# First pointwise product of a two-block transformer step: a new order for its operands, the diagonals and the first norm sums

## The chip, the core and the metric

The kernel runs on one core of one Trainium2 chip. A core has a matrix engine (TensorE, PE in the rows; PEld is its weight load), a vector engine (VectorE, DVE), an activation engine (ScalarE, ACT), a general engine (GpSimd, POOL) and an engine that here only issues transfers (SyncE, SP). Each works through its own instructions in the order in which the program was written, and they wait for each other by semaphores. The metric is device microseconds of one execution. Before the change three runs took 1481.81, 1485.37 and 1486.15 us, the median is 1485.37 us.

## The reference, cut to what matters

The program computes two blocks on 256 positions of 1024 channels in fp32. All that the change touches lies in the opening of the first block:

```python
c_act = silu(c)
mod = c_act @ mod_w + mod_b                      # 6 x 1024: shifts, scales, gates
sh_m, sc_m, gt_m, sh_f, sc_f, gt_f = split(mod)
h = rmsnorm(x, norm_pre_mix) * (1 + sc_m) + sh_m # x * rsqrt(mean(x^2) + eps) * g
u = h @ a_pw1_w + a_pw1_b                        # 1024 -> 2048, "first pointwise product"
a, gt = split(u)
u = a * sigmoid(gt)
u = causal_dwconv(u, a_dw_w) + a_dw_b            # 31 taps, depthwise
u = silu(layernorm(u, a_ln_g, a_ln_b))
x = x + gt_m * rmsnorm(u @ a_pw2_w + a_pw2_b, norm_post_mix)
...                                              # conv feed-forward, then the second block
```

## The kernel before

Everything is held with channels on the 128 partitions, in eight channel tiles of 256 positions (`xr` is x, `ys` work space). Products keep fp32 accuracy with two fp32r parts: an operand is split into a high part (a rounded copy) and a low part (the rest), and three matmuls high x high, high x low and low x high are summed. Weights come as 1 MB chunks (`wraw`, three buffers, `Stream.load`, L200). Each half chunk is split by ACT (`whi`, L226) and DVE (`wlo`, L235); when the second half has been split, SP is given the load of the chunk three further on (L238 to L241).

`pointwise_conv` (L915) is the opening. It goes like this:

- **Start.** PE runs matmuls that have no use but activity (`keep_warm`, L923; `WARM_START`, L31, says how many at four places), two matmuls that spread silu(c) over the partitions (L933), then more of the first kind. ACT squares x (L939); DVE adds the eight squared tiles up pairwise (L942 to L950), and two matmuls with one column sum over the partitions (L953). ACT and DVE make one over the root (L957, L975), PE transposes it (L977), ACT copies it to `rms` (L982).
- **Modulation.** One column of mod for a channel tile is a row of `mod_w` (`mraw`, 512 KB, five buffers) times silu(c) on DVE (`mod_mult`, L720) and a sum along the row on ACT (`mod_sum`, L724, an instruction and the readout of its accumulator). Each input tile k of the product needs two, shift and scale (`mult` and `sums`, L960 and L966). ACT's sum frees the buffer, and SP then loads a later row.
- **Product.** For each input tile k, PE does 48 matmuls (`pw1`, L1004): eight output tiles, two halves, three parts, into all eight PSUM banks. Its operand is made by DVE (`scaled`, L985, x times gain times rms), by DVE's add of a bias (L1031), by ACT (scale and shift, L1033; high part, L1034) and DVE (low part, L1045), and its weights by two splits.
- **Other work in the loop.** After k = 1 SP is given `taps` (L1051), the convolution's coefficients. After k = 2 POOL is given five instructions (`conv_stack`, L901) that each make 32x32 diagonal matrices of one channel tile out of the taps. After k = 5 SP is given `vecs`, the biases and gains, and `cst` (`load_consts`, L662).
- **Convolution.** ACT takes a sigmoid of each gate (L1099, with a bias out of `vecs`), DVE multiplies (`up`, L1101). PE makes shifted copies (L1072), ACT moves them (`sh`, L1076), and PE multiplies them with the diagonals (L1128) for seven channel tiles; the eighth is done by DVE, tap by tap (L1084, L1088). Between the taps DVE works on the 24 later rows of `mod_w`, ACT sums them; these are queued in `bg` and issued by `pump` while the convolution is written down. At its end come layer norm sums and the second pointwise product.

The order of all this is the order of the code: no scheduler moves anything. A DVE instruction that is written after a PE instruction does not wait for it unless it uses its data or a buffer that it holds.

## Time and profile before

| | |
|---|---|
| median of three runs | 1485.37 us |
| the profiled execution | 1481.87 us |
| its span (first to last instruction) | 1480.1 us |
| PE busy in the span | 1419.9 us (96%) |
| DVE, ACT, POOL busy | 1076.0, 853.8, 119.6 us |
| mean granted TensorE clock | 0.978 |

Of the span PE is busy nearly throughout, but the change is confined to the first 130 us. There the rows below are read: a timeline row gives the start, the busy time, the engine, the line of the code, the operation, output <- input and the number of instructions of a run; a bracket at its end gives the idle time of the engine before it and what ended it. A window row gives for a stretch its length, the busy time of engines, the granted clock of TensorE (1.00 is 2.4 GHz, 0.50 is 1.2 GHz), the share of the DMA engines' time and GB/s.

### The profile page before, as it was taken

Reading aid. Unit: us, or ns where it says so; the run is one execution under the profiler, and the core shown is the slowest. Engines: PE = TensorE matmul, PEld = TensorE weight load, DVE = VectorE, ACT = ScalarE, POOL = GpSimd, SP = SyncE. Lnnn points to the kernel's source line nnn. Section 1 sums busy time; section 2 is a strip of 40 time slices with the busy share of each in tenths; the row PEclk is TensorE's granted clock in tenths of the full one; section 3 lists DMA queues with packets and bytes.
Section 4 is the critical chain, followed back from the end, with each engine's and each line's share of the span. In section 5 each row is a group of like instructions: output and inputs, shape, how many; then the busy total and the mean of one; then the engine's idle time right before and its main releaser. Section 6 shows DMA issues by size and latency. Waiting matters only on the chain. (4 is left out here: it accounts for less than half of the span.)

```text
span 1480.1 us, 26075 instructions
## 1 busy us (share of the span) xinstructions
PE 1419.9 (96%) x10664; PEld 1273.4 (86%) x10664; DVE 1076.0 (73%) x1705; ACT 853.8 (58%) x1505; POOL 119.6 (8%) x113
## 2 busy tenths in 40 slices
PE   8888899999999999999999999999999999999997
PEld 7867799998888888898788888888888888888886
DVE  7897788885777656788568776678766765787754
ACT  6787566684655535751346555466554676565542
POOL 1210100001000010031010000110001111100011
PEclk9998899999999999999999999999999999999998
DMA  9774445565355553240024555536554342265540
GB/s 379 292 243 186 170 155 189 198 234 207 136 202 179 196 199 136 86 143 4 2 109 167 184 196 181 189 143 221 182 195 187 136 143 86 91 226 196 196 174 29
DMA packets 39145, 250.38 MB, mean 169 GB/s; under 512 B 4337, under 2 KB 4849, under 8 KB 12274
## 3 DMA queue, kind: packets, MB, share of 16 engines
q1 hardware_dynamic: 38594, 247.60, 45.9%
q8 instruction: 84, 1.38, 0.4%
q10 hardware_dynamic: 432, 1.11, 0.2%
q14 instruction: 35, 0.29, 0.1%
HBM read 247.65 MB, written 1.05 MB: 168 GB/s over the span
## 5 line engine op out<-in xcount | busy, mean ns | idle before, releaser
L235 DVE TENSOR_TENSOR wlo<-wraw,whi 128x1024 fp32r<-128x1024 f32 x416 | 514.3, 1250 | 34.1 <-ACT whi L226 33.4
L226 ACT CAST whi<-wraw 128x1024 fp32r<-128x1024 f32 x416 | 426.3, 1045 | 22.0 <-PE acc L378 5.6
L384 PE MATMUL acc<-hx,whi 128*128 128x512 f32 x880 | 310.7, 398 | 0.0
L384 PE MATMUL acc<-xx,whi 128*128 128x512 f32 x816 | 284.1, 390 | 0.0
L372 PE MATMUL acc<-xx,wlo 128*128 128x256 f32 x1008 | 280.7, 284 | 0.0
L372 PE MATMUL gu<-xx,wlo 128*128 128x256 f32 x1008 | 279.0, 282 | 1.6 <-ACT xx L625 1.0
L372 PE MATMUL acc<-hx,wlo 128*128 128x256 f32 x880 | 247.5, 281 | 0.0
L384 PEld LDWEIGHTS acc<-hx,whi 128*128 128x128 f32 x880 | 165.3, 188 | 40.5
L372 PEld LDWEIGHTS gu<-xx,wlo 128*128 128x128 f32 x1008 | 189.9, 189 | 4.9 <-ACT xx L625 1.7
L372 PEld LDWEIGHTS acc<-xx,wlo 128*128 128x128 f32 x1008 | 190.9, 191 | 0.8
L384 PEld LDWEIGHTS acc<-xx,whi 128*128 128x128 f32 x816 | 153.2, 188 | 32.1
L372 PEld LDWEIGHTS acc<-hx,wlo 128*128 128x128 f32 x880 | 166.1, 189 | 0.0
L384 PE MATMUL gu<-xx,whi 128*128 128x512 f32 x432 | 150.9, 390 | 0.0
L377 PE MATMUL gu<-xx,whi 128*128 128x256 f32 x512 | 148.4, 290 | 2.4 <-ACT u L894 2.4
L378 PE MATMUL gu<-xx,whi 128*128 128x256 f32 x512 | 142.9, 279 | 0.0
L1331 ACT ACTIVATE ys<-ys 128x256 f32<-128x256 f32 (+1 forms) x66 | 28.6, 437 | 151.7 <-DVE ys L1249 134.9
L377 PEld LDWEIGHTS gu<-xx,whi 128*128 128x128 f32 x512 | 96.2, 188 | 10.8 <-issue 7.9
L378 PEld LDWEIGHTS gu<-xx,whi 128*128 128x128 f32 x512 | 96.3, 188 | 0.7 <-issue 0.7
L384 PEld LDWEIGHTS gu<-xx,whi 128*128 128x128 f32 x432 | 81.1, 188 | 17.0
L1348 POOL TENSOR_TENSOR nsum<-ys 128x512 f32<-128x512 f32 (+1 forms) x9 | 12.4, 1380 | 871.1 <-PE acc L384 452.3
L858 ACT COPY lows<-acc 128x256 f32<-128x256 f32 x55 | 20.6, 374 | 97.8 <-PE acc L384 97.6
L1247 DVE SCALAR_TENSOR_TENSOR ys<-xr,acc 128x256 f32<-128x256 f32 x32 | 13.5, 422 | 75.0 <-PE acc L384 75.0
(397 smaller groups left out, 2351.5 us busy)
## 6 DMA issues: line engine op xcount, KB each, us to landing
wraw<-in_w SPq DMA_DIRECT2D x208, 1024.0 KB, 4.8
mraw<-in_mod SPq DMA_DIRECT2D x48, 512.0 KB, 5.5
xr<-in_x SPq DMA_DIRECT2D x2, 512.0 KB, 4.2
m<-in_mem SPq DMA_DIRECT2D x1, 1024.0 KB, 8.2
out<-xr SPq DMA_DIRECT2D x3, 256.0 KB, 2.2
cst<-in_consts SPq DMA_DIRECT2D x1, 546.0 KB
lora<-in_lora ACTq DMA_DIRECT2D x1, 384.0 KB, 3.4
lora_g<-in_lora ACTq DMA_DIRECT2D x1, 384.0 KB, 3.9
```

The source lines that it names most:

```text
L226: b.nc.scalar.copy(out=hi, in_=raw)
L235: b.nc.vector.tensor_tensor(out=lo, in0=raw, in1=hi.bitcast(F32), op=ALU.subtract)
L372: self.nc.tensor.matmul(out, lhsT=wl, rhs=x[:, 0, :], start=start, stop=False, skip_group_check=True)
L377: mm(out, lhsT=wh, rhs=x[:, 0, :], start=start, stop=False, skip_group_check=True)
L378: mm(out, lhsT=wh, rhs=x[:, 1, :], start=False, stop=False, skip_group_check=True)
L384: self.nc.tensor.matmul(bank, lhsT=wh, rhs=x, start=False, stop=stop, skip_group_check=True)
L858: nc.scalar.copy(out=lows[:, 1, :], in_=banks[1][:, 1, :])
L1247: self.nc.vector.scalar_tensor_tensor(out=y, in0=self.xr[:, k, :], scalar=2 * ALPHA, in1=ps[:, 1, :], op0=ALU.mult, op1=ALU.add)
L1331: b.nc.scalar.activation(out=b.ys[:, k0:k1, 1, :], in_=y, func=AF.Square)
L1348: e.tensor_tensor(out=out[:, q:2, :], in0=prev[:, q:2, :], in1=t[:, q:2, :], op=ALU.add)
```

## The change

The start's warm-up matmuls are cut from 10, 6, 3 and 24 to 10, none and 14, on another tile of the operand's low part. DVE's five adds of squares go; PE sums all eight squared tiles with 16 one-column matmuls in place of two. ACT's copy of the transposed root is written after both sums of the first modulation pair instead of between them. In the loop, a function `operand(k)` holds all that makes the operand and the weights of input tile k; it is called for k + 1 after the product of k is written. Within it, both modulation products come first on DVE, then `scaled`, and the two weight splits stand around the bias add; on ACT the two high parts of the weights stand before and after the two sums. `taps` are loaded after k = 6 and the five diagonals made after k = 7; `vecs` and `cst` are loaded after k = 6, which now is after `operand(7)`.

```diff
@@ -28,7 +28,7 @@
 CV = (5, 4)
 LOS = (1, 2, 3)
 MEMFILL = (4, 8, 2, 2)
-WARM_START = (10, 6, 3, 24)
+WARM_START = (10, 0, 14)
 CONV_ORDER = [4, 5, 0, 1, 2, 3, 6, 7]
 RWKV_PAIRS = [("zk", 0), ("zr", 0), ("zk", 1), ("zr", 1), ("zk", 2), ("zr", 2)]
 RWKV_FIRST = {"zr": 0, "zk": 6}
@@ -916,7 +916,7 @@
         nc = self.nc
         self.mod = self.const.tile([P, 48], F32, name="mod")
 
-        warm = self.xl[:, 0, :]
+        warm = self.xl[:, KD - 1, :]
         nc.vector.memset(warm.bitcast(F32), 0.0)
         junk = self.acc_tile(0)[:, 0, :]
 
@@ -939,20 +939,13 @@
             nc.scalar.activation(out=sq[:, k, :], in_=self.xr[:, k, :], func=AF.Square)
         self.preload(AF.Sqrt)
 
-        def add(i, j, n):
-            nc.vector.tensor_tensor(out=sq[:, i:i + n, :], in0=sq[:, i:i + n, :], in1=sq[:, j:j + n, :],
-                                    op=ALU.add)
-
         for h, ps in enumerate(rows):
             nc.vector.tensor_copy(out=self.cact[:, 512 * h:512 * h + 512], in_=ps)
-            add(4 * h, 4 * h + 2, 2)
-            add(4 * h, 4 * h + 1, 1)
-        add(0, 4, 1)
         st, bc = (self.ps_st.tile([P, 2, T], F32, name=nm, tag=nm) for nm in ("st", "bc"))
-        for h in range(2):
-            nc.tensor.matmul(st[:, 0, h:h + 1], lhsT=sq[:, 0, h * P:h * P + P], rhs=self.inv, start=True,
-                             stop=True, skip_group_check=True)
-        keep_warm(WARM_START[2])
+        for k in range(KD):
+            for h in range(2):
+                nc.tensor.matmul(st[:, 0, h:h + 1], lhsT=sq[:, k, h * P:h * P + P], rhs=self.inv,
+                                 start=k == 0 and h == 0, stop=k == KD - 1, skip_group_check=True)
         sd = self.tmp.tile([P, 2], F32, name="sd", tag="sd")
         nc.scalar.activation(out=sd, in_=st[:, 0, :2], func=AF.Sqrt, bias=self.epst[RMS_EPS])
         mods = {}
@@ -961,33 +954,28 @@
             mods[k] = [self.mod_raw.pop(0) for _ in range(2)]
             for r in mods[k]:
                 self.mod_mult(r)
-                yield
 
         def sums(k):
             for h, r in enumerate(mods.pop(k)):
                 self.mod_sum(r, h * KD + k)
-                yield
-            if self.n_mod < 2 * KD:
-                self.mod_load(2)
-
-        mult0, sums0 = mult(0), sums(0)
-        next(mult0)
+                if self.n_mod < 2 * KD:
+                    self.mod_load(1)
+
+        mult(0)
         nc.vector.reciprocal(out=sd, in_=sd)
         for h in range(2):
             nc.tensor.transpose(bc[:, 0, h * P:h * P + P], in_=sd[:, h:h + 1].to_broadcast([P, P]),
                                 identity=self.k("ident"))
-        keep_warm(WARM_START[3])
+        keep_warm(WARM_START[2])
         rms = cp.tile([P, T], F32, name="rms", tag="sg", bufs=2)
-        next(sums0)
+        sums(0)
         nc.scalar.copy(out=rms, in_=bc[:, 0, :])
-        next(mult0)
 
         def scaled(k, rms):
             nc.vector.scalar_tensor_tensor(out=self.ys[:, k, 0, :], in0=self.xr[:, k, :],
                                            scalar=self.vec("norm_pre_mix", k), in1=rms,
                                            op0=ALU.mult, op1=ALU.mult)
         scaled(0, bc[:, 0, :])
-        list(sums0)
         self.mark("pw1")
         bias = self.const.tile([P, 2, KD], F32, name="sbias")
         nc.vector.tensor_copy(out=bias[:, 0, :], in_=self.vec("mod_b", 0, 8))
@@ -1017,44 +1005,45 @@
             for t in todo:
                 products(*t)
 
-        for k in range(KD):
+        def operand(k):
+
             y, sh, sc = self.ys[:, k, 0, :], mod[:, 0, k:k + 1], mod[:, 1, k:k + 1]
             xh, xl = self.xh[:, k, :], self.xl[:, k, :]
             if k:
-                next(mults)
+                mult(k)
                 self.stream.split_hi()
+                sums(k)
                 self.stream.split_hi()
-                list(sums(k))
-                self.stream.split_lo()
                 scaled(k, rms)
                 self.stream.split_lo()
             nc.vector.tensor_tensor(out=mod[:, :, k], in0=mod[:, :, k], in1=bias[:, :, k], op=ALU.add)
             if k:
                 nc.scalar.activation(out=y, in_=y, func=AF.Identity, scale=sc, bias=sh)
                 nc.scalar.copy(out=xh, in_=y)
+                self.stream.split_lo()
             else:
                 self.stream.split_hi()
                 self.stream.split_hi()
                 for o in (xh, y):
                     nc.vector.tensor_scalar(out=o, in0=y, scalar1=sc, scalar2=sh, op0=ALU.mult, op1=ALU.add)
-                self.stream.split_lo()
-            if k < KD - 1:
-                mults = mult(k + 1)
-                if k:
-                    next(mults)
             nc.vector.tensor_tensor(out=xl, in0=y, in1=xh.bitcast(F32), op=ALU.subtract)
             if k == 0:
-                next(mults)
                 self.stream.split_lo()
+                self.stream.split_lo()
+
+        operand(0)
+        for k in range(KD):
             pw1(k)
-            if k == 1:
-                nc.sync.dma_start(out=self.taps, in_=self.dr["taps"])
-            elif k == 2:
-                stacks = [self.conv_stack(cp, j) for j in first[:N_STACK]]
-            elif k == 5:
+            if k < KD - 1:
+                operand(k + 1)
+            if k == 6:
                 self.load_consts()
             if k > 4:
-                self.mod_load(5 - len(self.mod_raw) - (k < KD - 1))
+                self.mod_load(5 - len(self.mod_raw))
+            if k == 6:
+                nc.sync.dma_start(out=self.taps, in_=self.dr["taps"])
+            if k == 7:
+                stacks = [self.conv_stack(cp, j) for j in first[:N_STACK]]
         self.preload(AF.Sigmoid)
         st = Norm(self, True)
         ups = [cp.tile([P, (3 if j >= ndv else CW - 1) + T], F32, name=f"up{j}") for j in range(KD)]
```

On PE, at the start (`acc_137<-xx` are the warm-up matmuls, `st<-inv,ys` the norm sums, `bc<-head,sd` the transposes), before and then now:

```order
L925 MATMUL acc_137<-xx 128x256 x10
L933 MATMUL gu<-cact,one_95 128x512 x2
L925 MATMUL acc_137<-xx 128x256 x6
L953 MATMUL st<-inv,ys 128x1 x2
L925 MATMUL acc_137<-xx 128x256 x3
L977 MATMUL bc<-head,sd 128x128 x2
L925 MATMUL acc_137<-xx 128x256 x24
```

```order
L925 MATMUL acc_137<-xx 128x256 x10
L933 MATMUL gu<-cact,one_95 128x512 x2
L947 MATMUL st<-inv,ys 128x1 x16
L967 MATMUL bc<-head,sd 128x128 x2
L925 MATMUL acc_137<-xx 128x256 x14
```

Six and three warm-up matmuls are gone and 14 one-column sums have been added, all ahead of the transposes.

On DVE, one round of the loop, in the middle of it (`mraw` is a modulation product, `ys<-xr,head,rms` is `scaled`, `wlo` a weight's low part, `mod` the bias add, `xx` the operand's low part), before and then now:

```order
L235 TENSOR_TENSOR wlo<-wraw,whi 128x1024
L986 SCALAR_TENSOR_TENSOR ys<-xr,head,rms 128x256
L235 TENSOR_TENSOR wlo<-wraw,whi 128x1024
L1031 TENSOR_TENSOR mod<-mod,sbias 128x2
L720 TENSOR_TENSOR mraw<-mraw,cact 128x1024
L1045 TENSOR_TENSOR xx<-ys,xx 128x256
L720 TENSOR_TENSOR mraw<-mraw,cact 128x1024
```

```order
L720 TENSOR_TENSOR mraw<-mraw,cact 128x1024 x2
L975 SCALAR_TENSOR_TENSOR ys<-xr,head,rms 128x256
L235 TENSOR_TENSOR wlo<-wraw,whi 128x1024
L1019 TENSOR_TENSOR mod<-mod,sbias 128x2
L235 TENSOR_TENSOR wlo<-wraw,whi 128x1024
L1029 TENSOR_TENSOR xx<-ys,xx 128x256
```

The seven instructions of a round are the same. Before, the two products stood behind the bias add, for the next round; now they stand at the head of their own round, and a split stands between the bias add and the low part.

On SP, the end of the product (with what each transfer waits for; `DVE_49` is DVE's split that frees the buffer), before, from the load of chunk 8, and then now, from the load of chunk 9:

```order
L204 DMA wraw<-in_w 128x2048 [waits DMAHW6_49,DVE_49]
L663 DMA vecs<-in_vecs 128x710 [waits DMAHW7_49]
L664 DMA cst<-in_consts 128x1092 [waits DMAHW0_49]
L733 DMA mraw<-in_mod 128x1024 [waits DMAHW1_49,Activation_49]
L204 DMA wraw<-in_w 128x2048 [waits DMAHW2_49,DVE_49]
L733 DMA mraw<-in_mod 128x1024 [waits DMAHW3_49,Activation_49]
L733 DMA mraw<-in_mod 128x1024 [waits DMAHW4_49,Activation_49]
L204 DMA wraw<-in_w 128x2048 [waits DMAHW5_49,DVE_49]
```

```order
L204 DMA wraw<-in_w 128x2048 [waits DMAHW7_49,DMAHW5_49,DVE_49]
L733 DMA mraw<-in_mod 128x1024 [waits DMAHW6_49]
L733 DMA mraw<-in_mod 128x1024
L733 DMA mraw<-in_mod 128x1024 [waits DMAHW0_49]
L204 DMA wraw<-in_w 128x2048 [waits DMAHW2_49,DMAHW1_49,DVE_49]
L663 DMA vecs<-in_vecs 128x710
L664 DMA cst<-in_consts 128x1092 [waits DMAHW3_49]
L733 DMA mraw<-in_mod 128x1024 [waits DMAHW4_49]
L733 DMA mraw<-in_mod 128x1024 [waits DMAHW5_49]
L1044 DMA taps<-in_taps 128x288 [waits DMAHW6_49]
```

The vectors stood behind the load of chunk 8, which waits for the splits of tile 5; now they stand behind that of chunk 10, which waits for the splits of tile 7. The taps, which had their place before the rows shown of before, are now last.

## Rows read from the trace of the kernel before

**Rows 1.** windows: stretch, us, busy us of PE PEld DVE ACT POOL, PEclk, DMA

```profile
17.00:73.00 56.00, 48.25 (x388) 47.20 (x387) 51.07 (x66) 40.13 (x65) 12.15 (x5) 0.94 0.88 339
...
73.00:120.00 47.00, 38.99 (x681) 28.88 (x680) 44.89 (x60) 39.50 (x75) 5.14 (x2) 0.96 0.72 238
```

**Rows 2.** timeline, PE, first pointwise product: start us, busy us, [idle before, releaser]

```profile
24.81 0.84 PE L1009 MATMUL gu<-xx,whi 128*128 128x256 f32 x2 [2.05 <-ACT xx L1034]
...
40.72 0.58 PE L1009 MATMUL gu<-xx,whi 128*128 128x256 f32 x1 [4.09 <-ACT xx L1034]
...
72.97 3.80 PE L1072 MATMUL gu<-up,head 128*32 128x256 f32 x64
```

**Rows 3.** timeline, POOL, the diagonals

```profile
32.41 12.15 POOL L906 TENSOR_TENSOR stack<-taps 128x1024 f32<-128x1024 f32 x5 [31.96 <-DMA taps<-in_taps]
```

**Rows 4.** timeline, DVE, slowed instructions (first and last of five)

```profile
32.81 2.14 DVE L986 SCALAR_TENSOR_TENSOR ys<-xr,head,rms 128x256 f32<-128x256 f32 x1
...
42.70 2.93 DVE L720 TENSOR_TENSOR mraw<-mraw,cact 128x1024 f32<-128x1024 f32 x1
```

**Rows 5.** windows, PE: stretch, us, busy us (matmuls), PEclk, DMA share, GB/s

```profile
24.80:36.70 11.90, 11.74 (x96) 1.00 1.02 411
...
40.70:47.60 6.90, 5.35 (x24) 0.52 0.44 161
```

**Rows 6.** timeline, DVE, one undisturbed round

```profile
46.69 0.47 DVE L986 SCALAR_TENSOR_TENSOR ys<-xr,head,rms 128x256 f32<-128x256 f32 x1
...
49.48 0.43 DVE L1045 TENSOR_TENSOR xx<-ys,xx 128x256 fp32r<-128x256 f32 x1
...
49.82 1.22 DVE L720 TENSOR_TENSOR mraw<-mraw,cact 128x1024 f32<-128x1024 f32 x1
...
50.96 1.22 DVE L235 TENSOR_TENSOR wlo<-wraw,whi 128x1024 fp32r<-128x1024 f32 x1
...
52.09 0.48 DVE L986 SCALAR_TENSOR_TENSOR ys<-xr,head,rms 128x256 f32<-128x256 f32 x1
```

**Rows 7.** timeline, ACT, the same stage

```profile
52.30 1.05 ACT L724 ACTIVATE mraw<-mraw 128x1024 f32<-128x1024 f32 x1
...
54.77 2.00 ACT L226 CAST whi<-wraw 128x1024 fp32r<-128x1024 f32 x2
```

**Rows 8.** timeline, all engines, the start; the last row is a later norm

```profile
7.47 1.65 PE L925 MATMUL acc<-xx 128*128 128x256 f32 x6
...
9.93 0.98 PE L953 MATMUL st<-inv,ys 128*128 128x1 f32 x4 [0.82 <-DVE ys L943]
...
10.95 0.26 ACT L957 ACTIVATE sd<-st,eps 128x2 f32<-128x2 f32 x1 [2.14 <-PE st L953]
...
11.84 5.23 PE L925 MATMUL acc<-xx 128*128 128x256 f32 x24
...
12.22 0.37 ACT L982 COPY rms<-bc 128x256 f32<-128x256 f32 x1
...
12.63 0.48 DVE L986 SCALAR_TENSOR_TENSOR ys<-xr,head,bc 128x256 f32<-128x256 f32 x1
...
120.33 1.05 PE L1383 MATMUL st<-inv,nsum 128*128 128x1 f32 x8 [1.70 <-DVE nsum L1348]
```

**Rows 9.** DMA: issue on SP; KB and us from issue to landing

```profile
54.32 0.42 SPq L663 DMA_DIRECT2D vecs<-in_vecs  x1
...
vecs<-in_vecs SPq DMA_DIRECT2D x1, 355.0 KB, 8.2
```

**Rows 10.** timeline, ACT and DVE, end of the product, start of the convolution

```profile
68.18 0.47 ACT L1099 ACTIVATE sg<-gu,vecs 128x256 f32<-128x256 f32 x1 [0.98 <-PE gu L1009]
...
73.98 0.41 DVE L1084 TENSOR_SCALAR ys<-up,vecs 128x256 f32<-128x256 f32 x1
```

**Rows 11.** waits, 73 to 122 us: us in total, times, longest

```profile
ACT mraw L724 <- DVE mraw L720: 3.0, 3, 2.2
...
DVE mraw L720 <- DMA mraw<-in_mod: 1.1, 3, 0.5
```


## The prediction

> **What bounds the kernel now.** I first read the windows, one for the product and one for the convolution. In the product (17 to 73 us) DVE is busy 51.1 of 56 us and PE 48.3; in the convolution (73 to 120 us) DVE is busy 44.9 of 47 us and PE 39.0 [rows 1]. So over both stages DVE comes nearest to being full, though PE fills the kernel as a whole. PE's timeline says when that shows: product 1 starts after an idle 2.05 us, product 3 after 4.09 us, each time on an operand that ACT delivers behind DVE [rows 2]. The second place is the larger one. There POOL makes the five diagonals, 12.15 us from 32.41 on, begun when the taps land [rows 3], and five DVE instructions take far longer than elsewhere: the first 2.14 us against 0.48, the last 2.93 against 1.22, so 1.66 and 1.71 too long, some 8.4 us for the five [rows 4, 6]. PE's idle time there also drops its clock: from 40.7 to 47.6 us the granted clock is 0.52, mostly the lower level of 1.2 GHz, and only 24 matmuls are done; before it, at 2.4 GHz, 96 matmuls (two products) take 11.7 us with the half microsecond of waits at their start, so a product is 5.6 to 5.9 us, and I use 5.6 [rows 5]. An undisturbed round of DVE takes 52.09 - 46.69 = 5.40 us [rows 6], a little less than a product.
>
> In the convolution ACT waits three times for DVE's modulation products, 3.0 us, and DVE waits only 1.1 us, for rows of mod_w [rows 11]. I read that stage as DVE's: what delays DVE there delays the sums on ACT, behind them the shifted copies, and the end.
>
> **The start.** PE sums eight tiles in place of one: 16 matmuls where there were 2. Those two show as four records, 0.98 us; eight of the later norm take 1.05 us [rows 8]. So 32 records cost 4.2 us at the quick rate and 7.8 at the slow one. The six warm-up matmuls just before take 1.65 us, 0.27 each, the slow rate of wide matmuls too; nothing after them will have sped PE up, so I stay near the slow end, with 0.22 each (the last of a run has no follower to hide it): 7.0 us. They can begin at 7.47 us, where the six began, and end at 14.5; before, the sums ended at 10.91 and the root began at 10.95 [rows 8]. DVE's adds fall away but were done by 9.93. From the root to the first `scaled` it was 12.63 - 10.95 = 1.68 us; now ACT's copy, which DVE followed at once, stands behind one more modulation sum of 1.05 us [rows 7, 8]. So `scaled` starts at 17.2 instead of 12.63. The warm-up of 24 that held PE to 17.07 no longer matters: what PE waits for comes later.
>
> From there DVE does, as I reckon, 1.9 us of small instructions (a `scaled`, the biases, the operand's parts, up to 0.5 us each), two splits (1.13 each by the starts) and, at about 21.4, the first product of round 1. Before the change that round's low part came at 24.8 with PE's product 1 [rows 2]; now it comes at 27.0, by the round that follows. That is 2.2 us late.
>
> **The round.** On DVE the same seven instructions stand in another order, and so the waits are others. The two products come first (1.14 and 1.22 us, so the second is ready at 2.36), then ACT's sum (1.05), its second weight part (1.0), and only then DVE's second split (1.13 to the next start) and the low part (0.34 to the next start) [rows 6, 7]: 2.36 + 1.05 + 1.03 + 0.04 + 1.13 + 0.34 = 5.95 us. Between the bias add and that split DVE has nothing to do; before, the next round's products filled that place. So a round now costs 0.55 us more than DVE's own 5.40 and also more than a product. That PE's next operand is "made while one runs" gains nothing by itself: DVE did not wait for PE's place in the code before either. Six further rounds from 27.0 end at 62.7, and the last product at 62.7 + 5.6 = 68.3; before, the next work of PE began at 72.97 [rows 2]. Without the diagonals the product is 4.7 us shorter, all of it less than the 8.4 us and the slow clock that it sheds.
>
> **The transfers behind it.** The sigmoids need `vecs`. That transfer now stands on SP behind the load that waits for the second split of tile 7, at about 62.9 us; nothing passes it. Ahead of it in the DMA engines are that 1 MB chunk and what is left of the chunk and three rows issued from 57 us on. At 411 GB/s [rows 5] these 2.6 MB run to about 64.8 us, the next chunk and `vecs` (1.4 MB) to 68.2, and with some delay to completion I put the landing at 69.5. Bounds: before, it took 8.2 us from issue to landing with two rows and a chunk ahead [rows 9], which gives 71.5; with nothing in its way it might land near 66. PE's first tile is done about 63.5. So the eight sigmoids (0.47 each [rows 10]) run from 69.5 to 73.3, ACT's and not PE's pace sets them, and DVE's first tap comes at 73.4; it was at 73.98 [rows 10]. Of the 4.7 us there are 0.6 left.
>
> **The diagonals.** `taps` come 1.8 MB after `vecs`, so about 73.7. The five instructions of POOL then run in the convolution, where DVE is again full, on instructions with the same kinds of operands (modulation products and taps, all from SBUF). I charge them what they cost before, 8.4 us. Their bounds are zero, if DVE's work in the convolution has slack, and 12.15, POOL's whole time [rows 3]. I take 8.4 because one of the slowed rows is a modulation product, which is most of what DVE does in the convolution. The 1.1 us that DVE waits for rows of mod_w there may be covered by it; I take off half, 0.6.
>
> The Trainium skill (SBUF — State Buffer, Who interferes with whom) says that a DVE instruction with two inputs in SBUF contends with a GpSimd instruction that reads SBUF, and that the loser of the shared port blocks for the other's whole instruction. By that rule the price would be 5 x 2.43 = 12.15 us instead of 8.4. The rows show the contention, but 1.7 us for each and not 2.43; the measurement decides, and the whole instruction is the rival below.
>
> **Sum.** -0.6 (start of the taps) + 8.4 (diagonals) - 0.6 (covered waits) = +7.2 us, all carried to the end, since the later stages are the same instructions. On the profiled execution, 1481.87 us (span 1480.1 and 1.8 around it), this gives 1489.1. The median of the runs is 3.5 us above that execution, so I say 1485.4 + 7.2 = 1492.6 us. Less than 0.3%, 4.5 us, can't be told from no change.
>
> **Rivals.**
>
> No change: the start is not late. If the norm sums run at the quick rate, 4.2 us, everything up to the taps comes 2.8 us earlier, and if `vecs` come with less queue, 1.5 more. For it: the same operation has that rate later. Against: the warm-up matmuls right before are slow. +7.2 - 4.3 = +2.9, 1488.3 us.
>
> Faster: the convolution hides the diagonals, because its end hangs on ACT and PE and DVE's 95% is only waiting work done early; and `vecs` come by 64 us, in time for PE. Both are needed: then the 4.7 us of the product stay, 1480.7 us. For it: PE waits in the convolution for ACT's copies and not for DVE directly. Against: ACT's longest waits there are for DVE. It decides from the point where less than 0.2 us of the 8.4 reach the end.
>
> Slower still: POOL holds the port for its whole instruction, 12.15 us, since in the convolution nearly every DVE instruction has two SBUF inputs. +7.2 + 3.7 = +10.9, 1496.3 us; the late first diagonals would also hold PE's convolution until 76 and could bring its clock down again as they did from 40.7 us.
>
> That the change doesn't do what it says is part of my forecast: the overlap in its name existed.
>
> **How the numbers follow.** My forecast 0.54, no change 0.22, faster 0.10, slower still 0.14. The forecast's own range is 1488 to 1497. Faster by over 0.3%: 0.09, from the faster case. Within 0.3%: 0.27, the no-change case and a small part of the forecast's lower edge. Slower: 0.64. The range of 8 in 10 runs from 1484, which leaves out most of the faster case, to 1499, which leaves out the tail of the last.
>
> **What would show it.** In the profile of the changed kernel: the root of the first norm starts near 14.5 us (11.7 would be the quick rate); product 1 near 27; rounds of DVE of 5.9 to 6.0 us with a wait of some 0.6 us for ACT's weight part; no DVE instruction of 2 us or more in the product, and the granted clock at 1.00 through it; the last product ending near 68; the first sigmoid waiting for a DMA until 69 to 71; five DVE instructions of the convolution some 1.7 us too long; the second norm's sums near 127 instead of 120.33. I am wrong if the convolution from DVE's first tap to that norm is no longer than before, or if the first tap comes at 70 or earlier.

## The result and the profile after

The changed kernel takes 1491.75 us (median of five runs, 1490.50 to 1493.19), the kernel before 1482.29 us (median of five, 1481.81 to 1486.15): a ratio of 1.0056, interval 1.0039 to 1.0073. It is slower, by 9.5 us. The profiled execution took 1493.19 us (span 1491.4), 11.3 us more than that of before. Two runs of the experiments further down, 1515.09 us in e2 at a granted clock of 0.899 and 2296.88 us in e8 at 0.556, are left out of the medians there.

The same places as in [rows 1 to 11], in the changed kernel. First the timeline of all engines, from the norm to the first taps:

```profile
7.47 6.99 PE L947 MATMUL st<-inv,ys 128*128 128x1 f32 x32
...
14.49 0.26 ACT L950 ACTIVATE sd<-st,eps 128x2 f32<-128x2 f32 x1 [5.69 <-PE st L947]
...
17.12 0.48 DVE L975 SCALAR_TENSOR_TENSOR ys<-xr,head,bc 128x256 f32<-128x256 f32 x1 [2.17 <-DMA wraw<-in_w]
...
26.98 0.39 PE L997 MATMUL gu<-xx,whi 128*128 128x256 f32 x1 [1.62 <-ACT xx L1022]
...
55.27 0.15 DVE L1019 TENSOR_TENSOR mod<-mod,sbias 128x2 f32<-128x2 f32 x1
55.98 1.23 DVE L235 TENSOR_TENSOR wlo<-wraw,whi 128x1024 fp32r<-128x1024 f32 x1 [0.56 <-ACT whi L226]
57.13 0.42 DVE L1029 TENSOR_TENSOR xx<-ys,xx 128x256 fp32r<-128x256 f32 x1
...
63.12 0.42 DVE L1029 TENSOR_TENSOR xx<-ys,xx 128x256 fp32r<-128x256 f32 x1
63.59 0.43 SPq L663 DMA_DIRECT2D vecs<-in_vecs  x1
...
69.06 0.28 PE L997 MATMUL bc<-xx,wlo 128*128 128x256 f32 x1
69.31 0.84 ACT L1088 ACTIVATE sg<-gu,vecs 128x256 f32<-128x256 f32 x2 [4.91 <-DMA vecs<-in_vecs]
...
73.59 16.48 POOL L906 TENSOR_TENSOR stack<-taps 128x1024 f32<-128x1024 f32 x7 [73.14 <-DMA taps<-in_taps]
```

Read from the top. The norm sums hold PE 6.99 us where the few of before took 0.98, and `scaled` starts at 17.12 instead of 12.63 [rows 8]. PE's product 1 starts at 26.98 (24.81 before, [rows 2]). A round of DVE is 63.12 - 57.13 = 5.99 us against 5.40 [rows 6], and the bracket at 55.98 shows why: 0.56 us of waiting for ACT's second weight part, in each round. The product ends at about 69.3 us, ahead of the 72.97 of [rows 2], but the first sigmoid waits 4.91 us for `vecs`, to 69.31, and the diagonals come only now.

DVE's timeline at the start of the convolution and at its end:

```profile
73.87 1.77 DVE L1073 TENSOR_SCALAR ys<-up,vecs 128x256 f32<-128x256 f32 x1
75.57 2.93 DVE L720 TENSOR_TENSOR mraw<-mraw,cact 128x1024 f32<-128x1024 f32 x1
78.42 2.13 DVE L1077 SCALAR_TENSOR_TENSOR ys<-up,vecs,ys 128x256 f32<-128x256 f32 x1
80.47 2.93 DVE L720 TENSOR_TENSOR mraw<-mraw,cact 128x1024 f32<-128x1024 f32 x1
83.33 2.13 DVE L1077 SCALAR_TENSOR_TENSOR ys<-up,vecs,ys 128x256 f32<-128x256 f32 x1
85.38 2.92 DVE L720 TENSOR_TENSOR mraw<-mraw,cact 128x1024 f32<-128x1024 f32 x1
88.22 2.12 DVE L1077 SCALAR_TENSOR_TENSOR ys<-up,vecs,ys 128x256 f32<-128x256 f32 x1
90.27 1.21 DVE L720 TENSOR_TENSOR mraw<-mraw,cact 128x1024 f32<-128x1024 f32 x1
91.40 0.47 DVE L1077 SCALAR_TENSOR_TENSOR ys<-up,vecs,ys 128x256 f32<-128x256 f32 x1
...
127.99 0.69 DVE L1337 TENSOR_TENSOR nsum<-nsum,ys 128x512 f32<-128x512 f32 x1 [0.48 <-ACT ys L1320]
```

As long as POOL works, seven instructions in a row are too long; the two rows from 90.27 on show the ordinary durations. Their excess is 1.36 for the first, against the 0.41 of [rows 10], three times 1.70 to 1.71 over 1.22, and three times 1.64 to 1.65 over 0.48: 11.42 us. Before, two diagonals fell into the convolution:

```profile
81.56 2.14 DVE L1088 SCALAR_TENSOR_TENSOR ys<-up,vecs,ys 128x256 f32<-128x256 f32 x1
...
85.58 2.63 DVE L720 TENSOR_TENSOR mraw<-mraw,cact 128x1024 f32<-128x1024 f32 x1 [0.34 <-DMA mraw<-in_mod]
...
119.59 0.69 DVE L1348 TENSOR_TENSOR nsum<-nsum,ys 128x512 f32<-128x512 f32 x1 [0.48 <-ACT ys L1331]
```

They cost 1.66 and 1.41, together 3.07, so the change adds 8.35 us there, nearly all of the 8.51 by which the way from the first tap to the last row above has grown (54.12 us, before 45.61). The windows of that way, after and then before, bear on a rival, that PE gets its diagonals late and DVE waits for PE:

```profile
73.90:128.00 54.10, 38.47 (x648) 26.93 (x648) 51.93 (x59) 38.38 (x74) 16.17 (x7) 0.94 0.61 205
```

```profile
74.00:119.60 45.60, 37.99 (x668) 28.19 (x658) 43.70 (x59) 38.62 (x74) 5.14 (x2) 0.96 0.74 244
```

DVE, whose last addition ends that way, is without work for 2.2 us of it after and 1.9 before. By the rival this idle time would have grown by the whole loss; it grew by 0.3 us.

DVE's last addition for the second norm, the mark that I use from here on, starts at 127.99 instead of 119.59: 8.40 us late. The same 8.4 us stand between the two kernels until 183 us.

The rest of the profiled difference arises between 183 and 319 us, in code that the change does not touch. Two table loads of ACT bound it: the first comes 8.41 us later than before, the second 10.99.

```profile
183.51 1.28 ACT L338 ACT_TABLE_LOAD   x1
...
318.92 1.28 ACT L338 ACT_TABLE_LOAD   x1
```

(Before: 175.10 and 307.93.) These 2.6 us come in two pieces. The first stands near 215 us, behind one and the same gap of PE. The windows around it, after and then before:

```profile
212.00:214.30 2.30, 0.01 (x1) 0.02 (x1) 2.18 (x6) 1.83 (x4) 0.00 (x0) 1.00 0.40 57
214.40:216.40 2.00, 2.00 (x13) 2.00 (x14) 2.00 (x3) 0.74 (x2) 0.00 (x0) 0.71 0.99 414
216.40:218.40 2.00, 2.00 (x12) 2.00 (x11) 1.13 (x4) 2.00 (x4) 0.00 (x0) 0.50 0.23 57
218.40:220.40 2.00, 2.00 (x18) 2.00 (x18) 2.00 (x5) 0.90 (x2) 0.00 (x0) 0.94 0.93 377
```

```profile
203.50:205.80 2.30, 0.00 (x0) 0.02 (x1) 2.17 (x6) 1.83 (x4) 0.00 (x0) 1.00 0.25 71
206.00:208.00 2.00, 2.00 (x19) 2.00 (x19) 2.00 (x3) 0.84 (x2) 0.00 (x0) 1.00 0.99 414
208.00:210.00 2.00, 2.00 (x20) 2.00 (x19) 1.13 (x4) 2.00 (x4) 0.00 (x0) 1.00 0.40 70
```

PE stood idle for 2.3 us in one and 2.4 in the other; after it the clock fell to the lower level, 0.50, in one execution and stayed at 1.00 in the other. The same 26 matmuls behind the gap take 4.67 us (from 214.31 to 218.98) instead of 3.11, so this piece is 1.6 us. The second piece follows with the granted clock at 1.00 in both: over 60 us of the stretch behind, PE does 512 matmuls after and 516 before.

```profile
248.92:308.92 60.00, 60.00 (x512) 1.00 0.52 183
```

```profile
237.93:297.93 60.00, 60.00 (x516) 1.00 0.52 194
```

That makes the remaining 0.9 to 1.0 us. The profiles of the experiments below have either piece, both or none. From the one load to the other it takes 132.6 to 132.8 us with none (before, e1, e4), 133.9 with the second alone (e3), 134.3 to 134.4 with the first alone (e2, e5, e6, e8, e9, e10) and 135.3 to 135.4 with both (e7 and the changed kernel). I see no pattern by edit, and why either piece appears stays open. So I compare kernels by what stands ahead of it, and by the medians.

### The profile page after: what moved, and what is told of

It reads as the page before. It is cut to its first block, busy times and chain, and to the rows that moved or that the text cites. A ratio compares the mean times of both kernels' runs of the same rounds, so it can differ in the third digit from the quotient of the medians.

```text
span 1491.4 us, 26081 instructions
## 1 busy us (share of the span) xinstructions
PE 1429.4 (96%) x10673; PEld 1281.3 (86%) x10673; DVE 1073.7 (72%) x1700; ACT 856.1 (57%) x1505; POOL 118.8 (8%) x113
## 3 DMA queue, kind: packets, MB, share of 16 engines
HBM read 247.65 MB, written 1.05 MB: 167 GB/s over the span
```

## The experiments

My theory: the loss is made by the late diagonals, which hold DVE 1.7 us each in the convolution, after three small delays (the start, the order of the round, `vecs`) have eaten what the product had gained. The rivals are named with each. "Sigmoid" is the start of the first sigmoid, "tap" that of DVE's first tap, "mark" that of the last norm addition, all in us of the profiled execution; "conv" is mark minus tap; "POOL" is the number of diagonals made within the convolution; "step" is the median less that of before in the same runs, in us.

| kernel | sigmoid | tap | mark | conv | POOL | median | step | ratio, interval |
|---|---|---|---|---|---|---|---|---|
| before | 68.18 | 73.98 | 119.59 | 45.61 | 2 | 1482.29 | | |
| changed | 69.31 | 73.87 | 127.99 | 54.12 | 7 | 1491.75 | +9.5 | 1.0056 (1.0039 to 1.0073) |
| e1 | 77.18 | 81.73 | 126.87 | 45.14 | 2 | 1492.30 | +9.2 | 1.0060 (1.0040 to 1.0080) |
| e2 | 64.46 | 70.31 | 124.00 | 53.69 | 7 | 1488.34 | +5.2 | 1.0041 (1.0028 to 1.0055) |
| e3 | 66.81 | 71.37 | 124.33 | 52.96 | 7 | 1488.39 | +5.0 | 1.0038 (1.0025 to 1.0052) |
| e4 | 59.68 | 65.48 | 118.67 | 53.19 | 7 | 1483.47 | +0.3 | 1.0002 (0.9990 to 1.0015) |
| e5 | 66.98 | 71.55 | 123.70 | 52.15 | 7 | 1487.45 | +4.0 | 1.0030 (1.0018 to 1.0042) |
| e6 | 70.58 | 75.14 | 120.19 | 45.05 | 2 | 1484.51 | +1.4 | 1.0007 (0.9996 to 1.0019) |
| e7 | 64.82 | 70.62 | 115.69 | 45.07 | 2 | 1479.61 | -3.8 | 0.9976 (0.9967 to 0.9986) |
| e8 | 69.46 | 74.03 | 119.61 | 45.58 | 7, written only | 1481.38 | -1.1 | 0.9990 (0.9979 to 1.0002) |
| e9 | 63.50 | 69.31 | 114.92 | 45.61 | 2 | 1478.11 | -4.4 | 0.9973 (0.9957 to 0.9989) |
| e10 | 65.14 | 70.95 | 116.37 | 45.42 | 2 | 1480.20 | -2.3 | 0.9981 (0.9969 to 0.9992) |

The column "conv" is the main finding: 45.1 to 45.6 us wherever two diagonals fall into the convolution, or seven that POOL only writes (e8), and 52.2 to 54.1 with seven. That e8 is no shorter than the runs with two has a reason of its own, told there.

**e1: the changed kernel, with taps and diagonals back in the product.**

```diff
+            if k == 0:
+                nc.sync.dma_start(out=self.taps, in_=self.dr["taps"])
+            if k == 1:
+                stacks = [self.conv_stack(cp, j) for j in first[:N_STACK]]
...
-            if k == 6:
-                nc.sync.dma_start(out=self.taps, in_=self.dr["taps"])
-            if k == 7:
-                stacks = [self.conv_stack(cp, j) for j in first[:N_STACK]]
```

> The changed kernel with only the taps' load and the five diagonals put back to where they were before (taps after the operand of tile 1, diagonals behind them, inside the product). My theory: DVE paces the product and the convolution alike, so the 8.4 us that POOL takes from DVE are paid in either stage; the product grows by 8.4, the vectors and the first tap come as much later (about 82 instead of 73.87), the convolution shrinks by 8.4, and the last norm sum of DVE stays near 128 (before 119.59, change 127.99): the time is that of the changed kernel, 7 to 10 us above the kernel before. Rival: it is the place in the convolution that costs (PE waits there for late diagonals), so the last norm sum falls back to 119.6 and the time to that of the kernel before, within 2 us.

The convolution is short again, by 9.0 us, and the product longer by nearly as much: the sigmoid comes at 77.18, 7.9 later, the mark only 1.1 earlier. The place of the diagonals alone decides little as long as DVE is full in both places.

**e4: the kernel before, with taps and diagonals at the end of the product, nothing else.**

```diff
-            if k == 1:
-                nc.sync.dma_start(out=self.taps, in_=self.dr["taps"])
-            elif k == 2:
-                stacks = [self.conv_stack(cp, j) for j in first[:N_STACK]]
...
+            if k == 7:
+                nc.sync.dma_start(out=self.taps, in_=self.dr["taps"])
+                stacks = [self.conv_stack(cp, j) for j in first[:N_STACK]]
```

> The kernel before with one part of the change: only the taps' load and the five diagonals moved to the end of the product. My theory: the product loses the stall and the slow clock, PE alone paces it from 24.8 on, 7 x 5.6 more, so it ends near 64 instead of 73; the first tap comes near 65 instead of 73.98; POOL then runs partly while DVE has nothing to do (from its last operand, near 57, to the first sigmoid), so that two or so of the five diagonals cost nothing and three cost 1.7 us each: last norm sum 115.5 to 119, the time 0.5 to 4 us below the kernel before. Rival: the late diagonals themselves are what makes the changed kernel slow; then this one is slower than the kernel before by 3 us or more.

The counterpart of e1. The product ends 8.5 us earlier and the convolution takes 7.6 longer; the mark is 0.9 earlier, the time the same. The gain of 0.5 to 4 us that I had expected did not come: the taps land so late that POOL starts at 66.34, behind the first tap at 65.48, and no diagonal falls into DVE's wait before it. So this part of the change is worth nothing by itself; what made the change slower is the rest.

**e2: the changed kernel, with the vectors loaded two tiles earlier.**

```diff
-            if k == 6:
+            if k == 4:
                 self.load_consts()
```

> The changed kernel with only the load of the vectors and constants put back ahead by two tiles (behind the chunk that waits for tile 5). My theory: the sigmoids no longer wait for a transfer, they start near 64.3 instead of 69.31 and then go at PE's pace, the first tap comes near 69.7 instead of 73.87, and the last norm sum near 124 instead of 127.99: 4 us off the changed kernel, so 3 to 6 us above the kernel before. Rival: the wait for the vectors is hidden behind something else (the diagonals or DVE's work), and the last norm sum stays within 1 us of 127.99.

The sigmoids no longer wait (first at 64.46, behind PE), the mark is 4.0 earlier, the step 4.3 smaller. The wait for `vecs` was real, but the diagonals stay.

**e3: the changed kernel, with the start of before** (DVE's five adds, two sums, the old warm-ups, ACT's copy of the root between the two modulation sums).

```diff
-WARM_START = (10, 0, 14)
+WARM_START = (10, 6, 3, 24)
...
+            add(4 * h, 4 * h + 2, 2)
+            add(4 * h, 4 * h + 1, 1)
+        add(0, 4, 1)
...
-        for k in range(KD):
-            for h in range(2):
-                nc.tensor.matmul(st[:, 0, h:h + 1], lhsT=sq[:, k, h * P:h * P + P], rhs=self.inv, ...)
+        for h in range(2):
+            nc.tensor.matmul(st[:, 0, h:h + 1], lhsT=sq[:, 0, h * P:h * P + P], rhs=self.inv, ...)
...
-        sums(0)
+        self.mod_sum(m0, 0)
         nc.scalar.copy(out=rms, in_=bc[:, 0, :])
...
```

> The changed kernel with only the start put back: 10, 6, 3 and 24 warm-up matmuls, the squares added on DVE, two norm sums, the copy of the transposed root between the two modulation sums. My theory: the root starts at 10.95 again instead of 14.49, the low part of tile 1 near 23.1 instead of 27.16, and all that follows, the load of the vectors too, as much earlier: first tap near 69.8, last norm sum near 124, 4 us off the changed kernel, 3 to 6 us above the kernel before. Rival: the start is hidden (PE's or the transfers' pace sets the rounds), and the last norm sum stays within 1 us of 127.99.

The mark is 3.7 earlier, the step 4.5 smaller: the new start was not free. This run takes back PE's norm sums and the place of ACT's copy together. `scaled` starts at 12.64 here, at 17.12 in the changed kernel and at 16.14 in e7 below, which has the sums but not the place of the copy; so about 3.5 us of the start are the sums and 1.0 the copy.

**e5: the loop order of before, with the rest of the change** (the start, the late taps, diagonals and vectors).

```diff
-            if k == 1:
-                nc.sync.dma_start(out=self.taps, in_=self.dr["taps"])
-            elif k == 2:
-                stacks = [self.conv_stack(cp, j) for j in first[:N_STACK]]
-            elif k == 5:
+            if k == 7:
                 self.load_consts()
             if k > 4:
                 self.mod_load(5 - len(self.mod_raw) - (k < KD - 1))
+            if k == 7:
+                nc.sync.dma_start(out=self.taps, in_=self.dr["taps"])
+                stacks = [self.conv_stack(cp, j) for j in first[:N_STACK]]
...
```

(against the kernel before; the start is edited as in the change)

> The changed kernel with the old order of the loop's instructions on DVE and ACT (the next tile's modulation products behind the bias add), everything else of the change kept: the start, the late taps, diagonals and vectors. My theory: rounds of DVE of 5.40 us instead of 5.99, without the wait of 0.56 us for ACT's second weight part; the low part of tile 7 near 60 instead of 63.1, the vectors' load and the first tap some 3 us earlier, the last norm sum near 125, 3 us off the changed kernel, 4 to 7 us above the kernel before. Rival: PE or the transfers pace the rounds, so the rounds stay near 6 us and the last norm sum within 1 us of 127.99.

Rounds of 5.41 us (low parts at 27.57, 32.98, 38.39), the mark 4.3 earlier, the step 5.5 smaller. The new order of the loop costs, too; nothing here shows a gain from it.

**e6: the changed kernel, with the five diagonals made at the very start.**

```diff
+            nc.sync.dma_start(out=self.taps, in_=self.dr["taps"])      # in setup, behind head
...
+        stacks = [self.conv_stack(cp, j) for j in [j for j in CONV_ORDER if j >= KD - N_PE_CONV][:N_STACK]]
         keep_warm(WARM_START[0])
...
-            if k == 6:
-                nc.sync.dma_start(out=self.taps, in_=self.dr["taps"])
-            if k == 7:
-                stacks = [self.conv_stack(cp, j) for j in first[:N_STACK]]
```

> The changed kernel with the taps loaded right behind x and the identity, and the five diagonals made at the very start, while DVE waits for the first norm (3.73 us of idle before its reciprocal). My theory: POOL slows at most DVE's two first modulation products, 1.7 us each, inside that idle time, and nothing later: the convolution sheds all 8.4 us, the last norm sum comes near 119.9 (0.3 for the taps' transfer), the time is that of the kernel before within 2 us. Rival: the diagonals cost about as much wherever they stand, since the start is on the path too; then the last norm sum stays above 125.

Nearly all of the loss goes: the mark is 7.8 earlier, the step 1.4 instead of 9.5. The diagonals are not quite free there. Two early modulation products take 4.56 us instead of 2.41, but inside DVE's wait for the norm; a copy of eight columns takes 1.33 instead of 0.17, and that puts the tap 1.3 later, at 75.14.

**e8: the changed kernel, with diagonals that POOL only writes.** It leaves out the diagonals' values: each becomes a memset behind a copy of one column of the taps, which holds it to its place.

```diff
-        self.nc.gpsimd.tensor_tensor(out=t, in0=eye..., in1=taps..., op=ALU.mult)
+        one = cp.tile([P, 1], F32, name="one_tap", bufs=N_PE_CONV)
+        self.nc.gpsimd.tensor_copy(out=one, in_=taps[:, j, :1])
+        self.nc.gpsimd.memset(t, 0.0)
```

> The changed kernel with the seven diagonals replaced by seven memsets of the same tiles on POOL, each behind a one-column copy of the taps that holds it to the same place (left out: the diagonals' values). Theory (POOL delays DVE where both read SBUF): no DVE instruction of the convolution above 1.5 us, the convolution some 8 us shorter, about 1484 us. Rival one (any POOL instruction on SBUF delays DVE): the taps and modulation products stay some 1.7 us too long, 1490 us or more unless the memsets are shorter themselves. Rival two (PE waits for the late diagonals, DVE's long rows are only a mark): DVE's rows go back to normal but the last norm add still starts at 126 or later, if POOL's seven take 16 us as before.

This asks whether it is POOL's reading beside DVE that costs, or that PE gets its diagonals late. POOL's and DVE's timeline of this run, the second and third of seven:

```profile
74.03 0.91 DVE L1074 TENSOR_SCALAR ys<-up,vecs 128x256 f32<-128x256 f32 x1
74.85 1.21 DVE L720 TENSOR_TENSOR mraw<-mraw,cact 128x1024 f32<-128x1024 f32 x1
74.90 0.95 POOL L908 MEMSET stack<- 128x1024 f32 x1
...
75.98 0.47 DVE L1078 SCALAR_TENSOR_TENSOR ys<-up,vecs,ys 128x256 f32<-128x256 f32 x1
76.04 0.95 POOL L908 MEMSET stack<- 128x1024 f32 x1
76.38 1.21 DVE L720 TENSOR_TENSOR mraw<-mraw,cact 128x1024 f32<-128x1024 f32 x1
```

Beside a memset DVE's rows are as short as without POOL; only the first tap is 0.5 too long. The memsets are also shorter than the diagonals (0.95 us), so PE's lateness shrinks with them, and this run does not part the two on its own; but DVE's rows are ordinary while POOL writes the same tiles, and the mark is back where it was before the change. What speaks against the lateness is DVE's idle time in the changed kernel's convolution, 2.2 us against 1.9 before, as shown with the result. The Trainium skill (SBUF — State Buffer, Who interferes with whom) says that DVE's instruction with two SBUF inputs contends with a GpSimd instruction that reads SBUF, not with one that only writes it; these rows agree.

Not all of the 11.42 us comes back: the convolution is 8.54 shorter, 45.58, the length of before, although no diagonal slows it. The waits of the convolution, in the changed kernel and then in e8, say why:

```profile
ACT mraw L724 <- DVE mraw L720: 11.8, 9, 3.8
...
DVE mraw L720 <- DMA mraw<-in_mod: 1.2, 1, 1.2
```

```profile
DVE mraw L720 <- DMA mraw<-in_mod: 3.6, 3, 1.6
...
ACT mraw L724 <- DVE mraw L720: 2.1, 3, 1.4
```

With DVE quick, ACT hardly waits for it any more, but the rows of mod_w become the limit: 3.6 us of waiting in place of 1.2. 11.4 less the tap's 0.5 and these 2.4 is 8.5.

**e7: what the runs before pointed to**: the loop order of before, PE's norm sums (with ACT's copy between the two modulation sums again), the diagonals at the very start, the vectors after k = 5.

```diff
-WARM_START = (10, 6, 3, 24)
+WARM_START = (10, 0, 14)
+            nc.sync.dma_start(out=self.taps, in_=self.dr["taps"])      # in setup, behind head
...
+        stacks = [self.conv_stack(cp, j) for j in [j for j in CONV_ORDER if j >= KD - N_PE_CONV][:N_STACK]]
         keep_warm(WARM_START[0])
```

(against the kernel before; the sums on PE as in the change)

> A mixture of both kernels: the changed start (16 norm sums on PE) with the copy of the root between the modulation sums, the diagonals made at the very start with the taps loaded behind x, and the old loop order with the old place of the vectors' load. My theory: tile 1 starts near 26.5, then PE alone sets the pace (5.6 us a tile) to about 65.7, the first tap near 66.7, and a convolution as long as before (45.6 us) gives the last norm sum near 112.3: 7 us below the kernel before, about 1475. Rival: the diagonals at the start delay DVE's first modulation products and the start with them, so that less than 3 us are left.

Faster than both kernels, by less than I had expected (a mark of 112.3 and 1475 us). DVE's timeline shows the first thing that I had not counted:

```profile
8.60 4.53 DVE L721 TENSOR_TENSOR mraw<-mraw,cact 128x1024 f32<-128x1024 f32 x2 [0.33 <-DMA mraw<-in_mod]
...
17.19 1.48 DVE L1025 TENSOR_TENSOR mod<-mod,sbias 128x2 f32<-128x2 f32 x1 [0.31 <-ACT mraw L725]
```

The two early products take 4.53 us instead of 2.41, which DVE has time for, but POOL's last diagonal still runs at 17.19 and makes an addition of two columns last 1.48 us instead of 0.16, on the path to the first product. The low part of tile 1 comes at 28.29, 1.8 later than worked out. The second is PE's clock: from 27.9 to 34.0 us it is 0.72 and PE does 32 matmuls, where e4, from 24.6 to 30.7, does 48 at 1.00. From the low part of tile 1 to the first tap it takes 42.3 us here and 40.8 in e4. The first tap is 3.9 us later than worked out (70.62 for 66.7), and these two are 3.4 of it.

**e9: e7, with the taps loaded ahead of x.**

```diff
             nc.sync.dma_start(out=self.cact[0:1, :], in_=self.dr["c"])
+            self.taps = self.modp.tile([P, 288], F32, name="taps", bufs=1)
+            nc.sync.dma_start(out=self.taps, in_=self.dr["taps"])
```

> The mixed version with the taps loaded in front of x, so that POOL can begin its five diagonals near 4 us instead of 7.30 and end near 15.4 instead of 18.65. Theory (what kept the mixed version from more is that the last of them held DVE's bias add, 1.48 us against 0.16, and two early modulation products, 4.53 against 2.41): first product 1.3 us earlier, low part of tile 1 at 27.0 instead of 28.29, last norm add at 114.4 instead of 115.69, about 1478.3 us. Rival (PE's norm sums to 14.46 and ACT's sums behind them set that place anyway, or x lands later behind the taps): 1479.6 to 1480.5 us.

```profile
3.43 11.34 POOL L908 TENSOR_TENSOR stack<-taps 128x1024 f32<-128x1024 f32 x5 [2.99 <-DMA taps<-in_taps]
...
14.79 0.17 DVE L971 RECIPROCAL sd<-sd 128x2 f32<-128x2 f32 x1 [1.79 <-ACT sd L953]
...
17.19 0.17 DVE L1026 TENSOR_TENSOR mod<-mod,sbias 128x2 f32<-128x2 f32 x1 [0.41 <-ACT mraw L726]
...
26.97 0.43 DVE L1040 TENSOR_TENSOR xx<-ys,xx 128x256 fp32r<-128x256 f32 x1
```

POOL is through at 14.8, before DVE is needed; the addition is short and the low part 1.32 us earlier, as worked out. The mark gains 0.8 of it. This is the fastest version, 1478.11 us, 4.4 below before in the same runs and, step against step, 13.8 below the changed kernel; its interval and that of e7 overlap.

**e10: the kernel before, with taps first and the diagonals at the very start, nothing else** (the two edits of e6 and e9, and the old places of both empty).

> The kernel before with its own start (norm tiles added by DVE), taps loaded first and the five diagonals made at the very start; nothing else changed. Theory (the diagonals are free only beside an idle DVE; in this start DVE works from 6.5 to 15 us, and they hold it some 1.7 us each for four of them): low part of tile 1 at 29 to 31 instead of 24.79, the rest as in the mixed version, 1479 to 1482 us. Rival (DVE has enough waits in the start to take them, since it waits for ACT and PE there): 25.5 to 27 at that place, 1475 to 1477 us, better than the mixed version.

In this start DVE has work: its first two adds take 4.26 us instead of 1.14, and the low part comes at 28.62 (24.79 before). It still beats the kernel before, since these 3.8 us are less than what five diagonals cost in the product.

## Why the prediction was right, step by step

- **Start.** Foretold 14.5 for the root and 17.2 for `scaled`; measured 14.49 and 17.12. The slow rate of the one-column sums, taken from the warm-ups beside them, held: 6.99 us against 7.0. e3 prices the new start as a whole.
- **The round.** 5.95 foretold, 5.99 measured, with the wait at the place named. PE's product 1 and low part at 26.98 and 27.16, for 27.0. e5 prices it. The last product ended at 69.3 instead of 68.3: 0.2 from the low part of tile 1, 6 x 0.04 from the rounds, and some 0.6 since I counted the 5.6 us from the start of the low part, while the matmuls that need it start when it has been written, 0.4 us later, and then take 0.2 longer. I had said that PE's clock would be 1.00 throughout; it was 0.86 in the first stretch, after the gaps at its start. That did not reach the end, since PE waited for the low part again in the last product (0.32 us):

```profile
24.80:36.70 11.90, 10.02 (x71) 9.61 (x70) 10.79 (x15) 10.09 (x17) 0.00 (x0) 0.86 0.96 350
36.70:69.20 32.50, 32.30 (x273) 31.82 (x271) 24.18 (x40) 24.06 (x39) 0.00 (x0) 1.00 0.88 327
```

- **`vecs`.** Foretold 69.5, the sigmoid started at 69.31. e2 shows that the wait ends last there. First tap 73.4 foretold, 73.87 measured: -0.1 instead of -0.6, because the sigmoids took 4.6 us to the tap and not 3.9: ACT waited three times among them, 0.7 us in all, for DVE's `up`. The 69.5 holds some luck. The sum for it does not come out as written: 2.6 MB from 57 us at 411 GB/s are through at 63.3 and not at 64.8. But the DMA engines moved only 300 GB/s from 57.2 to 63.2 us (420 from there to 69.4), which put the landing back near the forecast.
- **Diagonals.** +8.4 foretold by five slowed rows, of which [rows 4] shows the first and the last, 8.35 measured as seven rows less two. The rival with POOL's whole instruction as price (12.15) fell. So did the faster one: 8.4 us reach the mark, not 0.2. That PE's clock could fall again, as I had said beside the slower rival, it did: PE's timeline and the window behind it show 6.58 us without work and then the lower level.

```profile
90.82 1.53 PE L1061 MATMUL gu<-up,head 128*32 128x256 f32 x12 [6.58 <-ACT sh L1065]
```

```profile
90.00:95.00 5.00, 4.18 (x40) 2.13 (x44) 5.00 (x8) 3.98 (x8) 0.07 (x1) 0.50 0.50 182
```

  But DVE is busy all 5 us of it, and the mark is not later than DVE's own excess makes it.
- **Covered waits.** -0.6 foretold, none found: DVE waited 1.2 us for rows of mod_w where it was 1.1. e8 shows that this wait exists as a limit, 3.6 us, once DVE is quick.
- **Sum.** +7.2 foretold, +8.40 at the mark; the two missed terms (0.5 at the tap, 0.6 of cover) make the difference. The predicted time, 1492.6 us, is near the measured 1491.75 partly by luck of the base: I added 7.2 to a median of 1485.4, and the median of five runs is 1482.3. The measured step of 9.5 us is larger than mine, and I had no term for what arises between 183 and 319 us, 2.6 us in the profiled execution; how much of it is in the medians is not shown.

That the late diagonals were to blame for the whole loss, as one could read the +8.4, the runs refute: alone they change nothing (e4). The loss is that the product, with their 8.4 us gone, ended only 3.7 earlier and the first tap came 0.1 earlier, because the start, the order of the round and `vecs` each took some of it. Taken back one at a time they give 3.7, 4.3 and 4.0 us at the mark. These do not add up to 8.4 but to 12.0, since `vecs` stand behind the product's last splits and move with them; how they would share out with two taken back at once was not run.

## What to carry to other kernels

A helper on GpSimd that reads SBUF was free here only beside an idle VectorE: the same five instructions cost about 8 us in the product and in the convolution, 3.8 in the start of before, where VectorE works (e10), and 1.3 or less under the wait for the first norm. Seven memsets, which only write, made VectorE's rows 0.5 us longer in all (e8). Moving work from one full stage to another gained 1 us at most at the mark (e1, e4), however well the stage that it left then looked. And work that is moved to the end of a loop takes the transfers behind it along: a load of 355 KB, two tiles later, cost as much as a change of the loop's order.

## What the runs showed of the hardware

- The price of a diagonal to DVE does not depend on DVE's instruction: 1.7 us on one of 1.22 us, 1.66 on one of 0.48, and 1.3 (e7) to 1.7 (1.86 against 0.16 us at 37.73 in the kernel before) on an addition of 128x2 elements. POOL's own instruction lasted 1.92 us at 85.21 in the kernel before, and 2.35 on average in the seven of the changed kernel, with a busy DVE. That reads as if the two alternate and DVE waits out most of POOL's own time; the 12.15 us that I had priced as the whole contained POOL's own waits for DVE.
- A TENSOR_SCALAR with a single tensor in SBUF (beside its two columns of `vecs`) was held, too (1.77 us against 0.41), and by 0.5 us beside the first write-only memset and its one-column copy.
- One-column fp32 matmuls took 0.22 us a record at the start (32 in 6.99 us) and 0.13 in the second norm of the same run (8 in 1.05 us). The 14 warm-up matmuls behind the 32 were still slow, 0.24 us each (3.33 us), where those of the products take 0.12. The granted clock reads 1.00 there, from 7.47 to 18.5 us, so it does not show what made them slow.
- The same idle of PE, 2.3 to 2.4 us near 215 us, was followed by the lower clock in eight of the twelve profiles and not in the other four, at a cost of 1.6 us. At the start of tile 1's product it is the same: from 26.9 to 33.0 us the changed kernel shows 0.72 and 34 matmuls, e2 shows 1.00 and 47, though the two programs do not differ up to there. So the code alone does not decide it; what does is open.
- With the granted clock at 1.00, PE did 512 matmuls in 60 us in three profiles (changed, e3, e7) and 516 in the other nine, at the same place of the program. Why is open.
